# A hybrid decoder layer on one core: triangular inverses in seven small bundles instead of four, 16 narrow products a bundle in the preparation, another PSUM bank for the spatial gate, an undivided last tile, and other planner constants

## The chip, the cores and the metric

The kernel runs on one core of one Trainium2 chip. TensorE (PE) multiplies, VectorE (DVE) and ScalarE (ACT) work element by element and empty PSUM, GpSimd (POOL) does a few small things, and SyncE (SP) issues nearly all DMA transfers, in one queue and in program order. The metric is the device time of one execution in microseconds (us); the median of several runs counts, and less is better.

## What is computed

One layer of a decoder on 1024 tokens of width 2048: RMSNorm, one wide input projection, three groups that read its columns, an output projection, and a last RMSNorm. Cut to what matters here:

```python
h = rmsnorm(x, ln_g[l]);  proj = h @ w_in[l]          # 1024 x 2048 by 2048 x 6672
# group A: u * (tril(W_s) v + b) per chunk of 128 tokens, times silu(g_z)
s = jnp.einsum('gts,bcsgd->bctgd', w, v) + bs.T[None, None, :, :, None]
# group B: gated delta rule, 8 heads of 128, chunks of 64
a = jnp.where(strict, jnp.einsum('bhnid,bhnjd->bhnij', kb, k) * decay, 0.0)
T = lax.linalg.triangular_solve(a + eye, eye, left_side=True, lower=True, unit_diagonal=True)
value = jnp.einsum('bhnij,bhnjd->bhnid', T, vb)
_, o = lax.scan(step, s0, xs)                          # state carried from chunk to chunk
# group C: softmax attention of 4 heads into 256 memory tokens
mixed = jnp.concatenate([out_a, out_b, out_c], axis=-1)
return rmsnorm(x + mixed @ w_out[l], final_g)
```

What the change touches of this: the projection of h on the 16 columns d_a and d_b (the decays), the inverse T, the order in which group A and group B are worked, and the end of the output projection.

## The kernel before

**Wide products.** The input projection, the keys and values of the memory and the output projection are cut into pieces of 128 x 128 weights against 128 x 512 columns. Each float32 operand is split into a rounded high part and a rest (`lh`/`ll`, `lm` for the left side, `rhi`/`rlo` for the weights), and three products stand for one. The projections save products by a scheme with seven partial sums (`seven`, lines 1289 to 1348): sums and differences of two halves of the tokens (`hs_d`, `h0_d`, `hT_d`) against sums and differences of weight blocks. ACT makes `rhi` by a cast and DVE makes `rlo` by a subtraction, from `raw` (two buffers, filled by DMA) or from `kept` (four blocks that stay).

**Narrow products.** Two places use a fraction of the TensorE array. `prep1` (lines 825 to 853) handles the token tiles 4 to 7: it loads the rows of x into buffers named `kept`, `ut`, `states`, `steps` and `tblk`, scales and transposes them, forms the sums that the seven-sum scheme needs, and multiplies them with 32-column blocks of `abw` for d_a and d_b: 32 products for a token tile. `levels` (lines 1032 to 1107) builds the inverse of 32 triangular 128 x 128 matrices from inverses of their 32 x 32 diagonal blocks: 64 products of 32 x 32, then 96 more on the result of the first, then 32 of 64 x 64, then 32 more, with a copy out of PSUM after each. It runs twice, for the heads 0 to 3 (called a here) and 4 to 7 (b). Its results go to DRAM by small DMAs (`uhi`, `ulo`, `umid`), come back as `ut` (`load_u`, line 1109), and the scan of the delta rule (`scan_step`) multiplies with them.

**The order.** Nothing is issued as it is written. The kernel records every operation in a `Plan` (lines 63 to 397; all instructions carry the line 398, where the recorded calls are made), which lays them out engine by engine. `lay` runs the operations through a table of costs, taking on each engine the operation with the lowest key that is ready; `late` goes backwards from the end and gives each operation a due time, which is the key of the next pass; `issue` keeps the best of some passes and emits in that order. On the chip each engine then works its own list strictly in order. `together()` makes PE operations one bundle that nothing may split, `behind(op)` adds a dependence, and `rank` a class. STRETCH multiplies latencies on the way back, AHEAD says how far the modelled SP queue may run ahead of its transfers, PASSES counts the passes after the first.

**PSUM.** There are eight banks: `acc0` to `acc3` for the wide products, and `dn0` to `dn3` (dn_111 to dn_114 in the lists below) for the rest. The projection of the columns `zv` takes `acc` and dn2, dn3. `levels` takes dn0 and dn1, and `spatial` (the normalisation of group A's v, line 1620) takes dn1.

**The end.** The output projection's last bank is a tile of 128 tokens by 512 columns. Its last 24 products are made in two halves of 256 columns, so that the addition and the square sum of the first half run beside the products of the second; then `close` scales four column blocks and sends them out.

Of the kernel before, what the change touches and what calls it, by code (L numbers as in the profile page):

```python
# [17 lines left out]
P = 128  # L18
# [44 lines left out]
class Plan:  # L63
# [6 lines left out]
    FIRST, SPREAD, PASSES, STRETCH, AHEAD = 0, 1.75, 5, 1.0, 2000.0  # L70
# [112 lines left out]
    def price(self, o, name, outs, ins):  # L183
# [218 lines left out]
def kernel(  # L402
# [422 lines left out]
    def prep1(i):  # L825
# [20 lines left out]
        for q, (a, b, c, d, e) in enumerate(sets):  # L846
# [185 lines left out]
    def levels(gg, tdr, udr, n):  # L1032
# [19 lines left out]
        with rank(1):  # L1052
# [15 lines left out]
            for h in range(2):  # L1068
                turn_in(uhi[low(2 * h), :, low(0)], every(udr[64:96], h))
            with R.together():  # L1070
                for k in range(16):
                    for r in range(4):
                        t = tu[low(r), k] if r % 2 else tlo[low(r), k, low(0)]
                        PE.matmul(da[low(r), k], gc[low(r), k], t, start=True, stop=True)
            S.copy(yc, da)
            with R.together():
                for k in range(16):
                    for h in range(2):
                        r, q = low(2 * h), low(2 * h + 1)
                        PE.matmul(db[q, k], yc[r, k], tu[r, k], start=True, stop=True)  # L1080
                        PE.matmul(db[r, k], yc[q, k], uhi[q, k, low(1)], start=True, stop=True)
                        PE.matmul(da[q, k], tu[r, k], yc[r, k], start=True, stop=True)
            for h in range(2):
                S.copy(tlo[low(2 * h + 1), :, low(0)], da[low(2 * h + 1)])
                V.tensor_copy(uhi[low(2 * h), :, low(1)], db[low(2 * h)])
            S.copy(ux, db)
            sides = [(x_, h, w) for x_ in range(8) for h in range(2) for w in range(2)]
            with R.together():
# [73 lines left out]
    def heads_out(hf, hp, hss, rest):  # L1162
# [7 lines left out]
        for h, ob, bank in zip(hp, obs, scan_banks):  # L1170
# [4 lines left out]
            else:  # L1175
                e, y = sums(), ob.rearrange("p t c -> p (t c)")
# [112 lines left out]
    def seven(left, right, banks, takes, order, rows=False, last=False, first=0):  # L1289


        for n, key in enumerate(order):
# [3 lines left out]
            def product(t, i, a, ws, part=None, cols=None):  # L1296
                for u in range(2):
                    l, (hi, lo) = a[u], ws
                    o = bank[t]
                    if rows:  # L1300
                        l = [x_[:, t * P : (t + 1) * P] for x_ in l]
                        r = [x_[:, u * HT : (u + 1) * HT] for x_ in (hi, lo)]
                        if cols:
                            r, o = [x_[:, cols] for x_ in r], o[:, cols]
# [347 lines left out]
    tp = dnr.bufs[1]  # L1652
# [4 lines left out]
    tp = dnr.bufs[1]  # L1657
# [4 lines left out]
    for hf in range(2):  # L1662
        spatial(hf)
# [3 lines left out]
    el = over([abh[:, 0:HT], ring["tn"].bufs.pop()])  # L1667
    with rank(2.6):
# [107 lines left out]
    def total(r):  # L1776
        V.scalar_tensor_tensor(r[:, 4:5], r[:, 3:4], 1.0 / D, r[:, 4:5], op0=ALU.mult, op1=ALU.add)

    def close(half_, t):

        r, r0 = ssy[half_][t], half_ * HT + t * P
        total(r)
# [15 lines left out]
    def square(half_, t, c, cols=slice(0, HT)):  # L1798
        S.activation(jk[:, cols], ys[half_][t][c][:, cols], AF.Square, accum_out=ssy[half_][t][:, c : c + 1])
# [119 lines left out]
```

## Time and profile before

| | |
|---|---|
| median of 3 runs | 1586.66 us (1584.83 to 1587.31) |
| the profiled execution's own time | 1587.73 us |
| its span, first to last instruction | 1586.0 us |
| mean granted TensorE clock | 0.995 |
| DVE, ACT, POOL busy | 77%, 59%, 6% |
| DMA | 431.40 MB, mean 272 GB/s |

The span is what the trace shows; 1.73 us of the execution's own time lie around it. A matmul's duration in the trace is its time through the array; since matmuls are pipelined, the distance from one start to the next tells what one costs. The float32 products that are not rounded (32 x 32, 64 x 64, the `abw` blocks, transposes) appear as two or more records each.

### The profile page before, as it was taken

What the parts mean: (1) busy time and instruction counts of PE and PEld (TensorE: products, weight loads), DVE (VectorE), ACT (ScalarE), POOL (GpSimd) and SP (SyncE); (2) the same over time, 40 slices, a digit from 0 to 9 for tenths busy, and PEclk for the clock granted to TensorE, in tenths of its full rate; (3) what the DMA queues carried; (4) which work ended last, traced back from release to release, by engine and by line L of the source; (5) the groups of instructions that cost most, each with busy time, mean ns of one, the idle gap of its engine ahead of it and who ended that gap; (6) DMA issues with size and microseconds to landing.
All of it is one profiled execution on the core that took longest, in us unless ns stands there. A gap on an engine that the chain in (4) does not pass through costs nothing.

```text
span 1586.0 us, 25201 instructions
## 1 busy us (share of the span) xinstructions
PE 1559.0 (98%) x8773; PEld 1309.6 (83%) x8773; DVE 1219.6 (77%) x1802; ACT 931.7 (59%) x1921; POOL 102.1 (6%) x125
## 2 busy tenths in 40 slices
PE   8999999999999999999999999999999999999997
PEld 7987888888888778888888778888888888888886
DVE  6966844789979756887799667878668888688775
ACT  7832455767854247778864444876657864344455
POOL 0100001010020001110110010000000000000001
PEclk9999999999999999999999999999999999999999
DMA  9999866999988797886989896898868979678657
GB/s 328 305 333 330 288 182 201 323 324 336 301 260 275 236 294 245 263 282 193 276 275 319 240 261 218 279 343 284 257 211 267 310 263 351 214 269 294 227 151 274
DMA packets 338353, 431.40 MB, mean 272 GB/s; under 512 B 77353, under 2 KB 163890, under 8 KB 338226
## 3 DMA queue, kind: packets, MB, share of 16 engines
q1 hardware_dynamic: 336642, 427.09, 84.0%
q0 software_dynamic: 1088, 2.10, 0.4%
q8 instruction: 69, 1.13, 0.3%
q10 hardware_dynamic: 496, 0.61, 0.1%
q14 instruction: 58, 0.48, 0.1%
HBM read 330.29 MB, written 99.42 MB: 271 GB/s over the span
## 4 chain that ended last, share of the span: by engine, by line
PE 85%; DMA 4%; issue 1%; ACT 1%; DVE 1%; SPq 1%; POOLq 0%; POOL 0%; ACTq 0%; DVEq 0%
PE acc L398 53%; PE dn L398 32%; SPq L398 1%; DMA raw<-in_w_in_dram 1%; DMA E<-ed 1%; DMA late<-os 0%; DMA xr<-pd 0%; DMA kd<-late 0%; DMA ut<-uloa 0%; DMA ut<-in_x_dram 0%; DMA qT<-late 0%; DMA ll<-hsd 0%; ACT obs L398 0%; DVE tn L398 0%; ACT rhi L398 0%
## 5 line engine op out<-in xcount | busy, mean ns | idle before, releaser
L398 PE MATMUL acc<-lh,rhi 128*128 128x512 f32 x1024 | 396.6, 396 | 1.8 <-DVE obs L398 1.8
L398 PE MATMUL acc<-lh,rlo 128*128 128x512 f32 x1024 | 387.1, 396 | 0.2 <-DVE rlo L398 0.2
L398 ACT CAST rhi<-raw 128x1024 fp32r<-128x1024 f32 (+1 forms) x148 | 186.6, 1261 | 244.8 <-PE dn L398 119.3
L398 DVE TENSOR_TENSOR rlo<-raw,rhi 128x1024 fp32r<-128x1024 f32 (+1 forms) x148 | 219.3, 1482 | 106.6 <-ACT rhi L398 103.1
L398 PE MATMUL acc<-ll,rhi 128*128 128x512 f32 x688 | 269.9, 397 | 0.0
L398 PEld LDWEIGHTS acc<-lh,rhi 128*128 128x128 f32 x1024 | 193.3, 189 | 39.4 <-DVE obs L398 2.6
L398 PEld LDWEIGHTS acc<-lh,rlo 128*128 128x128 f32 x1024 | 193.0, 189 | 37.5 <-DVE rlo L398 0.7
L398 DVE TENSOR_TENSOR ll<-ll,lh 128x1024 fp32r<-128x1024 f32 x122 | 149.9, 1229 | 17.3 <-ACT lh L398 17.0
L398 PEld LDWEIGHTS acc<-ll,rhi 128*128 128x128 f32 x688 | 129.7, 189 | 24.8 <-DVE ll L398 0.2
L398 ACT CAST lh<-ll 128x1024 fp32r<-128x1024 f32 x122 | 127.9, 1048 | 23.2 <-DMA ll<-hsd 5.6
L398 PE MATMUL acc<-lm,rhi 128*128 128x512 f32 x336 | 133.4, 399 | 0.0
L398 PE MATMUL dn<-lh,rhi 128*128 128x512 f32 x288 | 112.9, 393 | 0.4 <-issue 0.4
L398 PE MATMUL dn<-lh,rlo 128*128 128x512 f32 x288 | 107.6, 393 | 0.0
L398 DVE TENSOR_TENSOR raw<-raw,kept 128x1024 f32<-128x1024 f32 (+1 forms) x56 | 81.1, 1452 | 3.6 <-DMA raw<-in_w_in_dram 3.6
L398 PE MATMUL dn<-ll,rhi 128*128 128x512 f32 x192 | 75.4, 394 | 0.0
L398 PEld LDWEIGHTS acc<-lm,rhi 128*128 128x128 f32 x336 | 63.6, 189 | 12.0
L398 DVE TENSOR_TENSOR rlo<-kept,rhi 128x1024 fp32r<-128x1024 f32 (+1 forms) x29 | 41.9, 1446 | 37.2 <-ACT rhi L398 37.1
L398 ACT CAST rhi<-kept 128x1024 fp32r<-128x1024 f32 (+1 forms) x29 | 35.7, 1230 | 51.4 <-PE dn L398 25.6
L398 POOL TENSOR_TENSOR hs<-hs,mhalf 128x4 f32<-128x4 f32 x32 | 45.8, 1436 | 273.7 <-DVE hs L398 262.6
L398 PEld LDWEIGHTS dn<-lh,rhi 128*128 128x128 f32 x288 | 54.3, 188 | 10.8
L398 PEld LDWEIGHTS dn<-lh,rlo 128*128 128x128 f32 x288 | 53.9, 188 | 10.4
L398 POOL TENSOR_TENSOR small<-small,mhalf 128x1 f32<-128x1 f32 x26 | 21.3, 819 | 580.7 <-DVE small L398 580.7
(412 smaller groups left out, 3395.8 us busy)
## 6 DMA issues: line engine op xcount, KB each, us to landing
raw<-in_w_in_dram SPq DMA_DIRECT2D x120, 512.0 KB
ll<-hsd SPq DMA_DIRECT2D x54, 512.0 KB
raw<-in_w_out_dram SPq DMA_DIRECT2D x48, 512.0 KB
raw<-in_w_in_dram SPq DMA_DIRECT2D x72, 256.0 KB
lm<-hsd SPq DMA_DIRECT2D x26, 512.0 KB
pd<-obs SPq DMA_DIRECT2D x48, 256.0 KB
late<-os SPq DMA_DIRECT2D x44, 256.0 KB
kept<-in_w_in_dram SPq DMA_DIRECT2D x20, 512.0 KB
```

The source lines that it names most:

```text
L398: o.fn(*o.args, **o.kw)
```

## The change

- **Inverses.** The four bundles of a `levels` (64, 96, 32 and 32 products) become seven of 32. The first 64 are halved, with a copy of half the bank after each half; the 96 are parted into three kinds, and each kind stands behind the copy of the one before it, so that other work can come between.
- **Preparation.** `prep1` closes its bundle after each half q: eight bundles of 16 in place of four of 32.
- **Spatial gate.** `spatial` and the transposes of its weights use dn2 instead of dn1, the names `scan_banks`, `hand`, `wide` and `el` are set before `spatial` runs, and `heads_out` takes its buffer from `E` instead of `sums`.
- **Last tile.** The last bank's products are 512 columns wide again; `close` computes the total by itself.
- **Planner.** PASSES 5 to 8, STRETCH 1.0 to 1.25, AHEAD 2000 to 1000, and a latency of 3500 more (FETCH) for products that are narrower than the array.

```diff
-    FIRST, SPREAD, PASSES, STRETCH, AHEAD = 0, 1.75, 5, 1.0, 2000.0
+    FIRST, SPREAD, PASSES, STRETCH, AHEAD = 0, 1.75, 8, 1.25, 1000.0
+    FETCH = 3500.0
...
-            o.lat = 175.0
+            o.lat = 175.0 + (0.0 if out.shape[0] == P or n == P or name == "transpose" else self.FETCH)
...
-        sets = [[pieces() for _ in range(5)] for q in range(2)]
-        for q, (a, b, c, d, e) in enumerate(sets):
+        for q in range(2):
+            a, b, c, d, e = (pieces() for _ in range(5))
...
-        with R.together():
-            for q, (a, b, c, d, e) in enumerate(sets):
+            with R.together():
                 for u, pair in enumerate(((c, a), (d, b))):
...
+            for e in range(2):
+                ks = slice(8 * e, 8 * e + 8)
+                with behind(R.ops[-1] if e else R.gate), R.together():
+                    for k in range(16)[ks]:
+                        for r in range(4):
+                            t = tu[low(r), k] if r % 2 else tlo[low(r), k, low(0)]
+                            PE.matmul(da[low(r), k], gc[low(r), k], t, start=True, stop=True)
+                S.copy(yc[:, ks], da[:, ks])
+            blocks = [(k, h, low(2 * h), low(2 * h + 1)) for k in range(16) for h in range(2)]
             with R.together():
-                for k in range(16):
-                    for r in range(4):
-                        t = tu[low(r), k] if r % 2 else tlo[low(r), k, low(0)]
-                        PE.matmul(da[low(r), k], gc[low(r), k], t, start=True, stop=True)
-            S.copy(yc, da)
-            with R.together():
-                for k in range(16):
-                    for h in range(2):
-                        r, q = low(2 * h), low(2 * h + 1)
-                        PE.matmul(db[q, k], yc[r, k], tu[r, k], start=True, stop=True)
-                        PE.matmul(db[r, k], yc[q, k], uhi[q, k, low(1)], start=True, stop=True)
-                        PE.matmul(da[q, k], tu[r, k], yc[r, k], start=True, stop=True)
+                for k, h, r, q in blocks:
+                    PE.matmul(da[q, k], tu[r, k], yc[r, k], start=True, stop=True)
             for h in range(2):
                 S.copy(tlo[low(2 * h + 1), :, low(0)], da[low(2 * h + 1)])
+            with behind(R.ops[-1]), R.together():
+                for k, h, r, q in blocks:
+                    PE.matmul(db[r, k], yc[q, k], uhi[q, k, low(1)], start=True, stop=True)
+            for h in range(2):
                 V.tensor_copy(uhi[low(2 * h), :, low(1)], db[low(2 * h)])
+            with behind(R.ops[-1]), R.together():
+                for k, h, r, q in blocks:
+                    PE.matmul(db[q, k], yc[r, k], tu[r, k], start=True, stop=True)
             S.copy(ux, db)
...
-            bank = dnr.bufs[1]
+            bank = dnr.bufs[2]
...
-                    if last and key == order[-1] and t == NT - 1:
-                        for cols in (slice(0, HT // 2), slice(HT // 2, HT)):
-                            for h in held:
-                                product(t, *h, cols=cols)
-                            takes[key](t, bank[t], cols)
-                        return
```

With other costs and constants the whole order changes, on every engine. Three places show it.

PE inside inverse a: before, the end of the bundle of 64, what stands between, and the start of the bundle of 96. The products of 32 x 32 read `gt`, `inv`; the wide ones write `acc`.

```order
L398 MATMUL dn_111<-gt_434,inv_432 32x32
L398 MATMUL dn_111<-inv_432 32x32
L398 MATMUL acc_110<-lh,rhi_76 128x512
L398 MATMUL acc_107<-lh,rhi_77 128x512
L398 MATMUL acc_107<-ll,rhi_77 128x512
L398 MATMUL acc_107<-lh,rlo_75 128x512
L398 MATMUL dn_112<-inv_432,inv_433 32x32
L398 MATMUL dn_112<-gt_435,inv_433 32x32
L398 MATMUL dn_111<-inv_433,inv_432 32x32
```

And now the same place, after the first bundle of 32, with the wide products in the middle left out:

```order
L399 MATMUL dn_111<-gt_434,inv_432 32x32
L399 MATMUL dn_111<-inv_432 32x32
L399 MATMUL acc_107<-lh,rlo_75 128x512
L399 MATMUL acc_107<-lh,rhi_77 128x512
L399 MATMUL acc_107<-lm,rhi_77 128x512
L399 MATMUL acc_107<-lh,rlo_75 128x512
...
L399 MATMUL dn_113<-lm,rhi_77 128x512
L399 MATMUL dn_113<-lh,rlo_75 128x512
L399 MATMUL dn_111<-gt_434,inv_432 32x32
L399 MATMUL dn_111<-inv_432 32x32
```

Four wide products stood between two bundles, now 18; between the other bundles of a and b there stand 18 to 25 products, nearly all of them wide (before 4 or 8 wide ones). After the last bundle of inverse a, 57 wide products and 8 of 128 columns stood before the first product of the scan that reads `ut`; now 73 and 8. After inverse b they were 434 and 64 (the spatial gate and more lay between), now 70 and 21.

DVE in the preparation, where the reduction for the row scale of the last token tile (`small_100`, which needs that tile's rows of x in `ut`) stands among the writes out of the transposes of the tile before it (`tn_86`, `tn_87`, `kT_350`, `kd_121` from the bank dn_112). Before:

```order
L398 TENSOR_TENSOR tn_86<-dn_112,gcol_130 128x512
L398 TENSOR_REDUCE small_100<-small_100 128x1
L398 TENSOR_SCALAR small_100<-small_100 128x1
L398 TENSOR_TENSOR rlo_75<-raw_73,rhi_77 128x1536
L398 TENSOR_TENSOR tn_87<-dn_112,gcol_130 128x512
L398 TENSOR_SCALAR ut_82<-ut_82,small_100 128x512
L398 TENSOR_TENSOR kT_349<-tn_86,tn_87 128x512
L398 TENSOR_SCALAR ut_83<-ut_83,small_100 128x512
L398 TENSOR_TENSOR kT_350<-dn_112,gcol_130 128x512
```

Now:

```order
L399 TENSOR_TENSOR tn_86<-dn_112,gcol_130 128x512
L399 TENSOR_TENSOR tn_87<-dn_112,gcol_130 128x512
L399 TENSOR_TENSOR kT_349<-tn_86,tn_87 128x512
L399 TENSOR_TENSOR rlo_74<-raw_72,rhi_76 128x1536
L399 TENSOR_TENSOR tn_86<-tn_88,tn_86 128x512
L399 TENSOR_TENSOR kT_350<-dn_112,gcol_130 128x512
L399 TENSOR_TENSOR tn_88<-kT_349,tn_88 128x512
L399 TENSOR_REDUCE small_100<-small_100 128x1
L399 TENSOR_TENSOR tn_89<-tn_89,tn_88 128x512
L399 TENSOR_TENSOR kd_121<-dn_112,gcol_130 128x512
```

The reduction stood ahead of three of the four writes out of that bank, now ahead of one. On SP the last of these rows of x is issued after 37.6 MB of transfers, before after 39.2 MB. On PE the narrow products of `prep1` form seven runs, not eight, since the first two bundles follow each other directly.

PE at the very end. Before, the last bank's first products, in half width:

```order
L398 MATMUL dn_114<-rlo_74,fh_521 128x512
L398 MATMUL dn_114<-rhi_76,fl_519 128x512
L398 MATMUL dn_111<-oh 128x256
L398 MATMUL dn_111<-rs,oh 128x256
L398 MATMUL dn_111<-oh,lm 128x256
```

Now:

```order
L399 MATMUL dn_114<-rhi_76,fl_519 128x512
L399 MATMUL dn_111<-rhi_77,ll 128x512
L399 MATMUL dn_111<-oh 128x512
L399 MATMUL dn_111<-rs,oh 128x512
L399 MATMUL dn_111<-oh,lm 128x512
```

24 products of 256 columns became 12 of 512.

More of the change, by code (lines that the diff above doesn't have):

```diff
@@ L1085, in levels @@
+            for h in range(2):
                 V.tensor_copy(uhi[low(2 * h), :, low(1)], db[low(2 * h)])
+            sides = [(x_, h, w) for x_ in range(8) for h in range(2) for w in range(2)]
+            with behind(R.ops[-1]), R.together():
+                for k, h, r, q in blocks:
+                    PE.matmul(db[q, k], yc[r, k], tu[r, k], start=True, stop=True)
             S.copy(ux, db)
-            sides = [(x_, h, w) for x_ in range(8) for h in range(2) for w in range(2)]
-            with R.together():
+            with behind(R.ops[-1]), R.together():
@@ L1294, in seven, with product @@
             bank = banks(key)
-            def product(t, i, a, ws, part=None, cols=None):
+            def product(t, i, a, ws, part=None):
                 for u in range(2):
@@ L1651 @@
     Q.dma_start(wt, gmlp_ws[0].rearrange("g t s -> t g s"))
-    tp = dnr.bufs[1]
+    tp = dnr.bufs[2]
     for g in range(NG):
@@ L1656 @@
         V.tensor_tensor(out=wsT[g], in0=tp[:, g * P : (g + 1) * P], in1=utri, op=ALU.mult)
[L1657 removed]
+    tp = dnr.bufs[2]
     for g in range(NG):
@@ L1661 @@
         V.scalar_tensor_tensor(bt[g], tp[:, sl], col2[:, 4 + g : 5 + g], bsb[:, sl], op0=ALU.mult, op1=ALU.add)
-    for hf in range(2):
-        spatial(hf)
     scan_banks = dnr.bufs[0:2]
@@ L1667 @@
     el = over([abh[:, 0:HT], ring["tn"].bufs.pop()])
+    for hf in range(2):
+        spatial(hf)
     with rank(2.6):
@@ L1846, in final, with take @@
             put = more(m, key, after)
-            def take(t, a, cols=slice(0, HT)):
-                r = ssy[key[0]][t]
-                if cols.stop - cols.start < HT:
-                    add(y[key][t][:, cols], a[:, cols], y[key][t][:, cols])
-                    square(key[0], t, c, cols)
-                    total(r) if cols.start == 0 else close(key[0], t)
-                    return
+            def take(t, a):
                 put(t, a)
                 square(key[0], t, c)
+                r = ssy[key[0]][t]
                 if c == 3:
```

13 lines of the change are left out of this document (4 added, 9 removed).

## The prediction

> **What bounds the kernel now.** First I read the page's busy shares and its chain of waits:
>
> ```profile
> PE 1559.0 (98%) x8773; PEld 1309.6 (83%) x8773; DVE 1219.6 (77%) x1802; ACT 931.7 (59%) x1921; POOL 102.1 (6%) x125
> PE 85%; DMA 4%; issue 1%; ACT 1%; DVE 1%; SPq 1%; POOLq 0%; POOL 0%; ACTq 0%; DVEq 0%
> ```
>
> PE is the bound, and nothing in the change takes wide products away. In an undisturbed stretch 24 of them take 5.44 us, 0.227 us each:
>
> ```profile
> 480.60 5.44 PE acc L398 x24
> ```
>
> So only PE's idle time, time at a lower clock, and the price of the narrow bundles can move. Second view: what PE waited for, in the whole run and in the windows of the two inverses (540 to 600, 890 to 930 us).
>
> ```profile
> PE dn L398 <- issue: 5.8, 5, 2.4
> PE dn L398 <- DMA ut<-uloa: 2.7, 1, 2.7
> PE acc L398 <- DVE obs L398: 1.8, 1, 1.8
> PE dn L398 <- DVE tn L398: 1.7, 1, 1.7
> ...
> PE dn L398 <- issue: 1.5, 2, 1.1
> ...
> PE dn L398 <- issue: 4.2, 3, 2.4
> ```
>
> All of the waiting on "issue" (1.5 + 4.2 = 5.7 us) lies in the two inverses: PE is held up by nothing that another engine does. The timeline of PE shows where, first in a, then in b:
>
> ```profile
> 554.84 0.21 PE L398 MATMUL dn<-gt,inv 32*32 32x32 f32 x1 [1.09 <-issue]
> 564.47 0.39 PE L398 MATMUL dn<-lh,rhi 128*128 128x512 f32 x1 [0.43 <-issue]
> ...
> 902.76 0.21 PE L398 MATMUL dn<-inv,inv 32*32 32x32 f32 x1 [2.40 <-issue]
> 908.95 1.16 PE L398 MATMUL dn<-gt,ut 64*64 64x64 f32 x64 [1.15 <-issue]
> 913.01 0.34 PE L398 MATMUL dn<-gt,inv 64*64 64x64 f32 x5 [0.70 <-issue]
> ```
>
> Third view: windows from the end of one such wait to the end of the next, and over the stretches at a lower clock.
>
> ```profile
> 902.75:908.94 6.19, 5.05 (x128) 3.70 (x128) 3.17 (x4) 1.74 (x3) 0.00 (x0) 0.72 0.85 267
> 908.94:913.00 4.06, 3.36 (x127) 2.70 (x127) 1.82 (x2) 2.48 (x3) 0.96 (x1) 1.00 0.65 189
> 554.84:564.46 9.62, 9.19 (x254) 7.15 (x255) 4.04 (x6) 3.55 (x7) 0.96 (x1) 0.82 1.04 325
> ...
> 556.18:559.59 3.41, 3.41 (x10) 2.46 (x8) 2.06 (x3) 1.74 (x3) 0.00 (x0) 0.50 1.06 344
> 580.08:583.49 3.41, 2.93 (x9) 2.57 (x10) 1.02 (x2) 0.96 (x3) 0.10 (x1) 0.50 1.17 262
> 904.34:907.75 3.41, 3.41 (x8) 2.16 (x8) 2.60 (x3) 1.67 (x3) 0.00 (x0) 0.50 0.88 259
> ```
>
> From wait to wait PE ran 128, 127 and 254 = 2 x 127 products, each with its weight load (the PEld column has as many). That is a supply that arrives in portions of 128 and needs 6.19, 4.06 and 9.62 / 2 = 4.81 us for one; wide products use a portion in 128 x 0.227 = 29 us, narrow ones in about 1. I read the waits as instruction supply. The last three rows show a second price: PEclk 0.50 for 3.41 us after each of these pile-ups and after the wait for `ut`, 1.7 us of lost work each.
>
> A sentence of the Trainium skill fits the portion: "Runtime: NRT & Kernel Launch", section "Instruction fetch mechanics", says that instructions are refilled in blocks of 256, which is 128 products with their weight loads. The same section calls the crossing of a block mostly hidden; by it the 5.7 us would have another cause and would stay (a rival below). The trace agrees on the block and not on the hiding.
>
> **The change part by part.** The sum starts from the profiled execution's own time, 1587.73 us (span 1586.0 plus 1.73 around it), which is 1.07 above the median.
>
> *Supply waits: -5.7.* Now each run is 32 products (64 records) followed by 18 to 25, nearly all wide: about 83 records in 0.55 + 20 x 0.227 = 5.1 us. At the slowest portion seen, 128 in 6.19 us, 105 would arrive in that time. So the supply keeps up. Bounds: 0 (nothing helps) and -5.7; I take -5.7, since 83 lies clearly under 105.
>
> *Clock: -3.4.* The two half-clock stretches behind these waits (556.18 and 904.34) cost 2 x 1.7. With half a microsecond of narrow work in 5 us PE looks like the rest of the run. Bounds 0 and -3.4; they go with the waits.
>
> *More bundles: +3.0.* A bundle costs something on entry and exit:
>
> ```profile
> 550.02 0.39 PE L398 MATMUL acc<-lh,rlo 128*128 128x512 f32 x1
> 550.34 0.21 PE L398 MATMUL dn<-gt,inv 32*32 32x32 f32 x1
> ...
> 551.44 0.19 PE L398 MATMUL dn<-inv 32*32 32x32 f32 x1
> 551.56 0.73 PE L398 MATMUL acc<-lh,rhi 128*128 128x512 f32 x2
> 552.13 0.39 PE L398 MATMUL acc<-ll,rhi 128*128 128x512 f32 x1
> ```
>
> In: 0.32 to the first narrow start instead of 0.227, 0.09 more. Out: 0.12, and the next two wide products take 0.57 instead of 0.45, 0.12 more. Together 0.33 us, with 0.4 as the upper bound for `abw` bundles, whose shape differs. There are 2 x 3 more in the inverses and 3 more in the preparation, nine in all: 9 x 0.33 = 3.0 (at most 3.6). This is paid on PE, with nothing beside it. The Trainium skill says the same against the change ("TensorEngine Tiling (Array Packing)", "Key Properties": a change of tiling mode drains the array) but gives no price; the trace's 0.33 is used.
>
> *Copies in the inverses.* One more PSUM copy and a longer row of hand-overs in each inverse. They lie beside 18 to 25 other products, so they cost PE nothing; without that cover each of the three added hand-overs would cost a copy of about 0.7 us:
>
> ```profile
> 561.02 0.69 DVE L398 COPY inv<-dn 128x512 f32<-128x512 f32 x1 [1.97 <-PE dn L398]
> ```
>
> *Scan behind the inverse: -3.4.* The result has to go out to DRAM and return before the scan.
>
> ```profile
> 563.08 0.50 PE L398 MATMUL dn<-lh,rlo 128*128 128x512 f32 x1
> ...
> 580.56 0.77 PE L398 MATMUL dn<-vs,ut 128*128 128x128 f32 x2 [2.70 <-DMA ut<-uloa]
> ```
>
> From the end of the last bundle to `ut` it took 580.56 - 563.08 = 17.5 us, and the 57 + 8 products in between did not fill it: 2.70 of wait and 1.7 of half clock, 4.4 in all. The new order puts 73 x 0.227 = 16.6 us there and 8 products of 128 columns, at most 0.60 / 4 = 0.15 each (the rows of x4 below): 16.6 to 17.8, about enough. But the scan now follows inverse b as closely: 70 x 0.227 and 21 smaller ones, 15.9 to 19.0 us (before 434 wide ones, so no wait there). Bounds: both covered, -4.4; both as bad as the one now, -4.4 + 8.8 = +4.4. I take half a microsecond of wait at each and no half clock, since the shortest wait that left half clock here was 1.09 us: -4.4 + 1.0 = -3.4.
>
> *Preparation: -1.7.* PE waited 1.72 us here (the chain of waits, first row, and the timeline):
>
> ```profile
> 119.00 5.78 DMA ut<-in_x_dram
> ...
> 125.62 0.16 DVE L398 TENSOR_REDUCE small<-small 128x1 f32<-128x4 f32 x1 [2.01 <-ACT jk L398]
> 128.67 0.68 DVE L398 TENSOR_TENSOR tn<-dn,gcol 128x512 f32<-128x512 f32 x1
> 129.41 0.66 PE L398 MATMUL dn<-ident,states 128*128 128x128 f32 x4 [1.72 <-DVE tn L398]
> 143.88 0.60 PE L398 MATMUL dn<-ident,ut 128*128 128x128 f32 x4
> ```
>
> DVE stood at the reduction for the last tile until its x had landed at 124.8, with `rlo` and the write `tn` queued behind it, for which PE waited to transpose again into that bank. The tile itself was wanted by PE only at 143.88, 19 us later. In the new order three of the four writes stand ahead of the reduction, and the last of x is issued after 37.6 MB instead of 39.2, which at 39.2 MB in 124.8 us is 5 us earlier. By the count of products ahead of it the preparation's last bundle comes 14 us of PE work earlier, so of the 19 us some 10 remain. Bounds: -1.7, and +1.7 (the wait stays and a second one joins it at the last write). I take -1.7, as the reduction's place in the queue was the cause.
>
> *Last tile: -0.7.* Before:
>
> ```profile
> 1573.84 0.28 PE L398 MATMUL dn<-oh 128*128 128x256 f32 x1
> ...
> 1576.18 0.39 PE L398 MATMUL dn<-oh 128*128 128x256 f32 x1 [0.74 <-DVE kd L398]
> ...
> 1577.59 0.28 PE L398 MATMUL dn<-rhi,fl 128*128 128x256 f32 x1
> 1577.91 0.42 DVE L398 TENSOR_TENSOR kd<-dn,kd 128x256 f32<-128x256 f32 x1
> 1578.72 0.42 ACT L398 ACTIVATE jk<-kd 128x256 bf16<-128x256 f32 x1 [0.53 <-DVE kd L398]
> ```
>
> The second half had to wait until the first was added out of the same bank. First to last start: 3.75 us; undivided 11 x 0.227 = 2.50, 1.25 earlier. Behind it the whole-tile steps are longer (rows for 512 columns):
>
> ```profile
> 1574.04 0.69 DVE L398 TENSOR_TENSOR kd<-dn,kd 128x512 f32<-128x512 f32 x1 [0.72 <-PE dn L398]
> 1574.83 0.63 ACT L398 ACTIVATE jk<-kd 128x512 bf16<-128x512 f32 x1
> ```
>
> 0.11 for the last product (0.39 against 0.28), 0.27 for the addition, 0.21 for the squares: +0.59. Net -0.66.
>
> *Bank of the spatial gate, `E`, planner constants: +4.0.* These have no price of their own: they move everything. The waits outside the inverses' "issue" are, start and end left aside, 2.7 + 1.8 + 1.7 and little else, so this order is good; a new one has waits of its own at other places. I have credited 1.7 and 3.4 for waits that go, and set +4.0 for ones that come; bounds 0 and +12, twice all the waits named here.
>
> Sum: -5.7 - 3.4 + 3.0 - 3.4 - 1.7 - 0.7 + 4.0 = -7.9, so 1579.8 for a profiled execution and, 1.07 lower, a median of about 1579.
>
> **Rivals.**
>
> *Both scans wait (slower).* The transfers of the inverses' last level stand in SP's queue behind writes that wait for DVE, and at b now also behind the spatial gate's. If a result takes longer than the middles of these stretches, 17.2 us at a and 17.5 at b, PE waits, and all behind it on PE. With one more transfer time on that way, like the 5.78 us of x in the preparation, it takes 23.3: waits of 6.1 + 1.7 at a and 5.8 + 1.7 at b, 15.3, less the 4.4 of now, +10.9 in place of -3.4. The median becomes about 1593. For it: 17.5 against 17.2 is no margin. Against: the results of the middle levels are now sent earlier.
>
> *The supply waits stay* (they belong to the modes, or 32 products are still too many): no -5.7 and no -3.4, about 1588, which cannot be told from no change. Against it: the portions of 127 and 128.
>
> *The new order has no new waits*: +4.0 falls away, and so does the wait for `obs` of 1.8 behind inverse b: about 1573.
>
> **How the numbers follow.** Forecast 0.55, no new waits 0.15, supply stays 0.12, both scans wait 0.18. Anything within 0.2% (3.2 us) cannot be told from no change: faster is below 1583.5. The forecast gives 0.51 of its 0.55 to faster and 0.04 to same; no new waits is faster; supply stays is same (0.09) or slower (0.03); both scans wait is slower. Faster 0.66, same 0.13, slower 0.21. All the best ends together give 1587.7 - 5.7 - 3.4 + 3.0 - 4.4 - 1.7 - 1.3 - 1.8 - 1.1 = 1571; the range reaches from a little below it, 1569, to the slower rival, 1593.
>
> **What would show it.** In the new profile the waits on "issue" should be near zero at the inverses and no 0.50 clock should stand there before the end; the bundles should show 0.33 us around each. A wait `ut` behind inverse a or b of more than 2 us, with half clock behind it, would show the slower rival. "issue" waits that stay, with 127 or 128 products between them, would refute the supply's balance; ones at other counts, the supply itself. A wait on `tn` or `kd` in the first 150 us would show the preparation wrong, and new waits on DVE or DMA of more than 10 us together the +4.0.

## The result and the profile after

| | before | after |
|---|---|---|
| median, same chip | 1587.19 us (1584.83 to 1589.31, 5 runs) | 1575.80 us (1574.23 to 1581.16, 5 runs) |
| ratio, 95% interval | | 0.9937 [0.9918, 0.9956] |
| the profiled execution's own time | 1587.73 us | 1575.80 us |
| its span | 1586.0 us | 1573.9 us |

The change makes the kernel faster by 11.4 us, or 0.6%, and the interval excludes a ratio of 1; about 1579 was predicted, with a range of 1569 to 1593. First the page of after: busy shares, the chain of waits, and one DMA queue to which we come back.

```profile
PE 1556.8 (99%) x8761; PEld 1307.4 (83%) x8761; DVE 1216.3 (77%) x1800; ACT 934.3 (59%) x1925; POOL 94.3 (6%) x125
PE 97%; DMA 1%; DVE 1%; issue 1%; ACT 1%; POOLq 0%; POOL 0%; ACTq 0%; SPq 0%; DVEq 0%
q8 instruction: 69, 1.13, 0.3%
```

The chain that ended last is PE's own work for 97% of the span, before for 85%. What is left between PE's products, in the view of waits (total us, times, longest):

```profile
PE dn L399 <- DMA y<-in_mem_norm_g_dram: 2.9, 1, 2.9
PE dn L399 <- issue: 1.7, 1, 1.7
PE dn L399 <- DMA kept<-in_mem_dram: 1.5, 1, 1.5
PE dn L399 <- ACT rhi L399: 1.0, 1, 1.0
PE dn L399 <- DVE states L399: 0.8, 1, 0.8
PE acc L399 <- ACT yu L399: 0.3, 1, 0.3
PE dn L399 <- ACT jk L399: 0.2, 1, 0.2
```

The waits on `y`, `kept` and `rhi` are the start of the kernel and stood in before as well. Those on `tn` and `obs` are gone, and "issue" is down from 5.8 in five to one of 1.7. The two inverses by windows, before and then after (columns: us, busy time of PE, PEld, DVE, ACT, POOL, granted clock, DMA share, GB/s):

```profile
549.00:567.00 18.00, 16.48 (x486) 12.86 (x485) 4.05 (x7) 5.72 (x9) 0.96 (x1) 0.91 0.94 260
896.00:914.00 18.00, 13.76 (x472) 10.53 (x472) 7.13 (x8) 6.43 (x9) 1.00 (x2) 0.91 0.82 216
```

```profile
540.10:578.00 37.90, 37.90 (x519) 30.56 (x519) 17.59 (x19) 11.93 (x14) 0.95 (x1) 1.00 1.01 313
924.00:965.00 41.00, 40.97 (x597) 32.50 (x596) 25.68 (x35) 21.95 (x32) 5.33 (x7) 1.00 0.81 227
```

An inverse is now stretched over more than twice the time, PE is busy in all of it, and the clock is 1.00 instead of 0.91. In the whole span of after no stretch at half clock is left but the one at the end.

The one "issue" that remains lies at the scan behind inverse a (timeline of PE):

```profile
572.38 1.16 PE L399 MATMUL dn<-gt,inv 64*64 64x64 f32 x64
...
590.88 0.39 PE L399 MATMUL dn<-lh,rhi 128*128 128x512 f32 x1
...
593.00 0.68 PE L399 MATMUL dn<-vs,ut 128*128 128x128 f32 x4 [1.73 <-issue]
```

Its name misleads. The product reads `ut`, the inverse's result, which comes in packets under 512 bytes; the DMA view of 592.0 to 592.5 and of 592.5 to 592.9 us shows when they stop:

```profile
DMA packets 147, 0.10 MB, mean 191 GB/s; under 512 B 114, under 2 KB 114, under 8 KB 147
...
DMA packets 41, 0.08 MB, mean 196 GB/s; under 512 B 3, under 2 KB 3, under 8 KB 41
```

The last of them ends at about 592.6, and PE starts at 593.00. So this is the wait for the result's way through DRAM, 1.73 us.

### The profile page after: what moved, and what is told of

Read it like the earlier page. It is cut to its first block, busy times and chain, and to the rows that moved or that the text cites. A ratio compares the mean times of both kernels' runs of the same rounds, so it can differ in the third digit from the quotient of the medians.

```text
span 1573.9 us, 25104 instructions
## 1 busy us (share of the span) xinstructions
PE 1556.8 (99%) x8761; PEld 1307.4 (83%) x8761; DVE 1216.3 (77%) x1800; ACT 934.3 (59%) x1925; POOL 94.3 (6%) x125
## 3 DMA queue, kind: packets, MB, share of 16 engines
q8 instruction: 69, 1.13, 0.3%
## 4 chain that ended last, share of the span: by engine, by line
PE 97%; DMA 1%; DVE 1%; issue 1%; ACT 1%; POOLq 0%; POOL 0%; ACTq 0%; SPq 0%; DVEq 0%
PE acc L399 59%; PE dn L399 38%; DMA raw<-in_w_in_dram 1%; ACT rhi L399 0%; DMA kept<-in_mem_dram 0%; DVE lm L399 0%; DVE raw L399 0%; DVE states L399 0%; ACT jk L399 0%; DVE inv L399 0%; ACT lh L399 0%; ACT vs L399 0%; DVE os L399 0%; ACT obs L399 0%; DVE kd L399 0%
## 5 line engine op out<-in xcount | busy, mean ns | idle before, releaser
L399 PE MATMUL acc<-lh,rlo 128*128 128x512 f32 x1024 | 380.2, 394 | 0.0
L399 PEld LDWEIGHTS acc<-lm,rhi 128*128 128x128 f32 x336 | 63.2, 188 | 11.9
L399 DVE TENSOR_TENSOR lm<-lm,lh 128x1024 fp32r<-128x1024 f32 x42 | 51.1, 1218 | 7.3 <-ACT lh L399 7.3
```

What stands on the lines that cost most here:

```text
L399: o.fn(*o.args, **o.kw)
```

## What the instruction queue shows

The page has a DMA queue for instructions, q8. Its 69 transfers are 1.13 MB / 69 = 16.4 KB each, and 8761 products with as many weight loads, shared among 69, are 254 instructions or 127 products: one transfer is one of the prediction's portions. The count can be made exact with the semaphore instructions that PE's queue holds as well: the stops of before at 902.76, 908.95 and 913.01 us stand at its instructions 10689, 10945 and 11201, 256 apart each time. All 15 waits on "issue" in before and in experiments 1, 3, 4 and 5 stand at 192 or 193 past a multiple of 256; no other wait of PE in the fourteen kernels does. Three windows of the kernel before: 900.3 to 901.3, 902.76 to 906.5 and 906.5 to 907.6 us.

```profile
q8 instruction: 1, 0.02, 6.0%
...
q1 hardware_dynamic: 1316, 1.29, 98.9%
...
q8 instruction: 1, 0.02, 5.6%
```

PE starts on one portion at 902.76 and runs dry within the next few microseconds, but for 3.8 us nothing comes on q8: the kernel's own transfers on q1 hold 98.9% of the DMA engines. The portion passes at 906.59 to 907.57, and PE goes on at 908.95. The trace has every transfer's time; some of them, with the products counted from border to border:

| kernel, inverse | PE enters a portion | the next passes on q8 | PE enters it | wait "issue" |
|---|---|---|---|---|
| before, b | 902.76 | 906.59 to 907.57 | 908.95 | 1.15 |
| before, b | 908.95 | 910.58 to 911.55 | 913.01 | 0.70 |
| experiment 1, a | 561.27 | 565.58 to 566.51 | 567.84 | 0.92 |
| experiment 3, a | 571.44 | 577.43 to 578.53 | 580.09 | 4.39 |
| experiment 5, a | 552.91 | 556.58 to 557.51 | 558.83 | 4.34 |

Every one of these waits ends 1.3 to 1.6 us after its transfer. The transfer itself takes 0.9 to 1.1 us, and it starts 1.6 to 6.0 us after PE entered the portion before. So a portion costs 4.1 to 8.7 us in these narrow stretches, and only one is fetched ahead: PE stands still when it gets through 128 products in less. In all fourteen traces PE enters no portion sooner than 1.3 us after its transfer. That the late starts come from the kernel's own data is likely but not shown: q1 held 96% and more of the DMA engines in the four long ones (3.7 to 6.0 us) and 82% in the short one.

The Trainium skill, "Runtime: NRT & Kernel Launch", section "Instruction fetch mechanics", describes an engine that fetches blocks of 256 instructions over a DMA queue of its own. The trace agrees on both. That crossing a block is mostly hidden holds here where wide products fill a block (29 us) or thin the narrow ones out, as in after, and not in before's inverses.

## The experiments

The kernel before ran beside each; on these chips its medians were 1583.6 to 1586.1 us, so ratios are compared. Single runs of one kernel spread over up to 8 us, so that a profiled run can stand 4 us from its kernel's median: the profiles of 1 and 12 are among the fastest of their twelve runs (1580.87 against a median of 1584.84, 1581.53 against 1584.28), that of 10 is the slowest of six (1581.09 against 1578.00).

**1. The seven bundles alone** (before, with the change's lines in `levels` and the old constants):

```diff
+            for e in range(2):
+                ks = slice(8 * e, 8 * e + 8)
+                with behind(R.ops[-1] if e else R.gate), R.together():
...
+            with behind(R.ops[-1]), R.together():
+                for k, h, r, q in blocks:
+                    PE.matmul(db[r, k], yc[q, k], uhi[q, k, low(1)], start=True, stop=True)
```

> The kernel before, with only the seven smaller bundles in the two inverses and the old planner constants: the bundles are 7 x 64 records with only 3 to 7 wide products between two of them. Supply theory (portions of 128 products, one in 4.1 to 6.2 us): 448 narrow and some 31 wide records would take PE about 11 us; in the kernel before the first wait came after 204 to 213 records, so some 270 are left, 2.1 portions, 8.5 to 13 us: 1.5 to 5 us of wait on issue in each inverse, with 127 or 128 products from one to the next, and a stretch of half clock behind the longest. Time 1584 to 1593, no gain over before. Rival (it is the length of a bundle or the number of levels in one mode that stops PE): no issue wait in either inverse, and 1587.2 - 5.7 - 3.4 + 2.0 (six more entries and exits) = about 1580.

Measured: ratio 1.0005 [0.9996, 1.0014]. The timeline, and the windows from wait to wait:

```profile
561.27 0.31 PE L398 MATMUL dn<-inv,inv 32*32 32x32 f32 x8 [0.93 <-issue]
567.84 0.34 PE L398 MATMUL dn<-inv,inv 32*32 32x32 f32 x10 [0.92 <-issue]
572.73 0.39 PE L398 MATMUL dn<-gt,inv 64*64 64x64 f32 x10 [0.28 <-issue]
910.99 0.33 PE L398 MATMUL dn<-gt,inv 64*64 64x64 f32 x6 [0.57 <-issue]
```

```profile
561.26:567.83 6.57, 5.65 (x128) 4.34 (x127) 4.15 (x6) 1.16 (x2) 0.00 (x0) 1.00 1.03 364
567.83:572.72 4.89, 4.61 (x127) 3.44 (x127) 1.29 (x2) 1.18 (x2) 0.96 (x1) 1.00 1.03 288
```

Small bundles do not end the waits: 128 and 127 products again. The 2.1 us in a were expected (1.5 to 5), the 0.6 in b are less, and no half clock followed in this profile. Its mean clock was 0.999, that of the eleven other runs 0.994 to 0.997, so they may well have had some. The rival, no such wait and a gain of 7 us, is out.

**2. No spacing** (after, FETCH at 0):

```diff
-    FETCH = 3500.0
+    FETCH = 0.0
```

> The kernel after, with the constant FETCH at 0, so that the planner puts only 3 to 11 wide products between the seven bundles of an inverse in place of 18 to 25. Supply theory: the issue waits come back, 1 to 5 us in each inverse, 127 or 128 products (or a multiple) from one to the next, and with them up to 1.7 us of half clock each: 1575.8 + 3 to 12 = 1579 to 1588. Rival (small bundles alone were enough): no issue wait in the inverses, 1575.8 within 3.

Measured: 1.0003 [0.9994, 1.0012], the whole gain lost, but with no wait on issue: the supply theory missed the kind of wait and the rival the time. The view of waits has others:

```profile
PE dn L399 <- DMA vd<-sm: 3.2, 1, 3.2
...
PE dn L399 <- DVE gt L399: 2.5, 2, 1.3
```

PE now waits 1.3 and 1.1 us for the copies between two bundles, and 3.2 behind inverse b, at the first product that reads its `ut`. While PE waits for the copies, portions pass: three of them end 1.4 to 1.5 us before their border is crossed, just in time, as in the table. So the spacing has two jobs, to let portions come and to cover the copies; here the waits for the copies seem to hide those for the portions. What the spacing alone is worth against the supply, this run does not show.

**3. Spacing alone** (after, with the old four bundles):

```diff
+                for k in range(16):
+                    for r in range(4):
...
+                        PE.matmul(db[q, k], yc[r, k], tu[r, k], start=True, stop=True)
+                        PE.matmul(db[r, k], yc[q, k], uhi[q, k, low(1)], start=True, stop=True)
```

> The kernel after, with the four bundles of before in each inverse (128, 192, 64 and 64 records), but the planner's spacing kept: 19 to 25 wide products between two. Supply theory: the stock at the start held 204 to 213 records in the kernel before, and 4.3 us pass between the first two bundles, about one portion; so 128 + 19 + 192 = 339 records meet a stock of some 205 and one portion more, 333: at most one short wait in each inverse, 0 to 2 us, at the end of the second bundle. Six entries and exits fewer give back 2.0 us. Time 1572 to 1579. Rival (the length of a bundle is what counts): a wait of 1 to 2.4 us stays in the bundle of 192 of both inverses, with half clock behind it, 1575.8 - 2.0 + 2 x (1.1 to 2.4 + 1.7) = 1579 to 1582.

Measured: 0.9976 [0.9966, 0.9986], slower than after. Inverse a has one long wait, b none. The row, and then the windows of the portion ahead of it and of the like one in b:

```profile
580.09 0.25 PE L399 MATMUL dn<-gt,inv 32*32 32x32 f32 x1 [4.39 <-issue]
```

```profile
571.43:580.08 8.65, 4.27 (x129) 3.40 (x127) 0.69 (x1) 0.00 (x0) 0.00 (x0) 0.86 0.99 304
944.50:951.52 7.02, 5.92 (x152) 4.76 (x141) 2.26 (x4) 2.12 (x3) 0.33 (x1) 1.00 0.58 159
```

Neither expectation fits whole. My count of a stock and portions on top was wrong: what counts is where the borders fall. In a, one portion held 12 wide products and 116 narrow ones and was gone in 4.1 us, while the next needed 8.7 with DMA at 0.99. In b a border fell into the first bundle, the next portion had the wide products and a wait for `inv` in it, and arrived in time. (The 152 of that row count also the records under way at its ends; from start to start it is 128.)

**4. The kernel before with the new constants:**

```diff
-    FIRST, SPREAD, PASSES, STRETCH, AHEAD = 0, 1.75, 5, 1.0, 2000.0
+    FIRST, SPREAD, PASSES, STRETCH, AHEAD = 0, 1.75, 8, 1.25, 1000.0
+    FETCH = 3500.0
...
+            o.lat = 175.0 + (0.0 if out.shape[0] == P or n == P or name == "transpose" else self.FETCH)
```

> The kernel before with the planner constants of after (FETCH among them) and nothing else: bundles of 128, 192, 64 and 64 records with 19 to 28 wide products between two. Supply theory: the issue waits of 5.7 us fall to 0 to 2 in all and both half-clock stretches in the inverses go, 1587.2 - 5.7 - 3.4 = 1578, with up to 4 us for what the redrawn order does elsewhere: 1576 to 1584. Rival (it is the bundles' length): the waits stay, 1585 to 1590.

Measured: 1.0034 [1.0022, 1.0046], slower than before; a miss. Both bundles of 192 records break:

```profile
551.47 0.26 PE L399 MATMUL dn<-inv,inv 32*32 32x32 f32 x2 [2.31 <-issue]
894.63 0.26 PE L399 MATMUL dn<-inv,inv 32*32 32x32 f32 x2 [3.28 <-issue]
```

A bundle of 192 can hold a whole portion, and the spacing around it did not help here. That is the sense in which the length of a bundle counts: not by itself, but against 128. The redrawn order also brought waits of 7.0 us elsewhere, 3.8 of them for `ll` at 424 us.

**5 and 6. The borders moved by half a portion,** in before and in after: 64 records more at the start, nothing else moved. The 32 products are work that neither kernel has otherwise.

```diff
+    with rank(0), R.together():
+        for k in range(32):
+            PE.matmul(dnr.bufs[1][0:32, 32 * (k % 16) : 32 * (k % 16) + 32], ident[0:32, 0:32], ident[0:32, 0:32], start=True, stop=True)
```

> The kernel before with 32 narrow products more (64 records of 32 x 32, about 1.1 us of PE, their result is not used) at the very start, everything behind them in the old order: each block border of 128 products falls 64 records earlier in the program, so half a block away from where it was. Supply theory: the waits on issue leave their places (products 81 and 72 of the second bundle) and come where the borders now are: at products 15 and 143 of the second bundle of inverse a and, with a fetch of 3.9 to 6.6 us for a block that PE goes through in 2.7 and 1.3 us, they are longer: 4 to 11 us in each inverse, 8 to 20 in all in place of 5.8, ratio to before 1.002 to 1.010. Rival (the waits belong to the bundles or their modes): the waits stay at products 81 and 72 with their lengths, ratio 1.000 to 1.001.

> The kernel after with the same 32 narrow products (result not used) at the start and the order else unchanged. Supply theory: a block in its inverses takes PE 7 to 12 us wherever the borders fall, longer than the 3.9 to 6.6 us of most fetches: no wait on issue in the inverses or one of at most 1.5 us; ratio to before 0.9937 + 0.0007 = 0.9944, within 0.002. Rival (the change was lucky with its borders): waits of 2 us and more with half clock behind them, ratio 0.997 to 1.001.

Measured: 1.0015 [1.0005, 1.0025] and 0.9952 [0.9938, 0.9966]. The waits of the shifted kernel before, and the window between the first two:

```profile
552.91 0.21 PE L398 MATMUL dn<-inv,inv 32*32 32x32 f32 x2 [0.67 <-issue]
558.83 0.21 PE L398 MATMUL dn<-inv,inv 32*32 32x32 f32 x1 [4.34 <-issue]
904.72 0.26 PE L398 MATMUL dn<-inv,inv 32*32 32x32 f32 x2 [4.76 <-issue]
```

```profile
552.90:558.82 5.92, 1.58 (x128) 1.46 (x128) 0.00 (x0) 0.00 (x0) 0.00 (x0) 0.94 1.02 330
```

The waits moved with the borders, in a to products 17 and 145 of the second bundle (15 and 143 expected, 81 before), in b to 136 (72 before), and grew from 5.8 to 9.8 us. This is the clearest of the runs: the same bundles, copies and order, and only the borders elsewhere. A price of the bundles or of their modes cannot move so. The time rose less than expected, as the wait for `ut` behind a fell from 2.70 to 0.65 meanwhile and the added products fit into a wait at the start. The shifted kernel after has no wait in its inverses and none for `ut`:

```profile
PE dn L399 <- DMA sm<-gvd: 0.6, 1, 0.6
PE acc L399 <- ACT yu L399: 0.3, 1, 0.3
PE dn L399 <- ACT jk L399: 0.2, 1, 0.2
```

Bundles of 64 records with some 20 wide products between held in both positions of the borders, and in the other orders below.

**7. Spatial gate as before** (bank, buffer and place in the program), and **9. its bank alone:**

```diff
-            bank = dnr.bufs[2]
+            bank = dnr.bufs[1]
...
-    tp = dnr.bufs[2]
+    tp = dnr.bufs[1]
```

> The kernel after with the spatial gate on its old bank, its old place in the program and the old buffer for its factor. Theory (the bank has no price of its own, it only lets the order be drawn otherwise): no issue waits in the inverses, waits at other places of 0 to 6 us, ratio 0.992 to 0.998. Rival (the bank of its own is what lets the scan follow inverse b closely and spares the wait for obs): that wait of 1.8 us comes back and others with it, ratio above 0.998.

> The kernel after with the spatial gate's products on the old bank and nothing else undone. The planner draws another order with it: between inverse b and the scan stand again some 460 wide products, behind inverse a 14.2 us of products. Supply theory: seven bundles with 19 to 27 wide products between, so no wait on issue over 1.5 us in either inverse. Waits of the order: the result of an inverse took 14.8 to 19.6 us from the last bundle to the scan in the runs so far, so 0.6 to 5 us of wait behind a, none behind b; and waits at other places as in the orders seen so far, 3 to 15 us in all. If the bank is what made the run with three things undone slow, the ratio is above 1.002; if it was that one order, 0.992 to 1.000.

Measured: 1.0074 [1.0060, 1.0089] and 1.0054 [1.0039, 1.0070]. The first was too slow for my theory, and its rival's mechanism did not come either: no wait on `obs`. In the second the bank is all that was undone, and it is enough. Its largest waits:

```profile
PE dn L399 <- ACT os L399: 7.0, 2, 3.5
...
PE acc L399 <- ACT rhi L399: 2.0, 1, 2.0
PE dn L399 <- ACT kd L399: 1.0, 1, 1.0
```

They lie at 393 and 403, at 67 and at 415 us, ahead of inverse a and far from the spatial gate: the planner drew another order, with a some 50 us earlier in PE's work and b 112 us of products ahead of its scan. All three kernels that have the old bank and the new constants (4, 7 and 9) wait for ACT or DVE between 360 and 435 us, none of the others does for 0.2 us.

**8. The last tile in halves** (after, with before's loop over `cols`):

```diff
+                        for cols in (slice(0, HT // 2), slice(HT // 2, HT)):
+                            for h in held:
+                                product(t, *h, cols=cols)
+                            takes[key](t, bank[t], cols)
```

> The kernel after with the last tile in two halves of its columns as before, the order of all else unchanged. Theory: from the first product of the last tile to the end of the span 12.18 us as in the kernel before, against 11.52 in after, +0.66, with the wait for the first addition of 0.74 back; ratio 0.9937 + 0.0004. Rival (the halves do not matter or help, as they let the last steps start earlier): 11.5 or less.

Measured: 0.9957 [0.9940, 0.9974]. From the first product of the last tile to the end 1572.93 - 1561.01 = 11.92 us, with this wait in it:

```profile
1563.35 0.39 PE L399 MATMUL dn<-oh 128*128 128x256 f32 x1 [0.74 <-DVE kd L399]
```

In five halved kernels that stretch takes 11.9 to 12.2 us, in the nine whole ones 11.5 to 11.8: whole is better by 0.4 or a little more; the ratio is too coarse for that.

**10, 11 and 12. One other edit undone each:** the factor's buffer, the preparation, and the three old constants beside FETCH.

```diff
-                e, y = ring["E"](), ob.rearrange("p t c -> p (t c)")
+                e, y = sums(), ob.rearrange("p t c -> p (t c)")
```

```diff
-        for q in range(2):
-            a, b, c, d, e = (pieces() for _ in range(5))
+        sets = [[pieces() for _ in range(5)] for q in range(2)]
+        for q, (a, b, c, d, e) in enumerate(sets):
```

```diff
-    FIRST, SPREAD, PASSES, STRETCH, AHEAD = 0, 1.75, 8, 1.25, 1000.0
+    FIRST, SPREAD, PASSES, STRETCH, AHEAD = 0, 1.75, 5, 1.0, 2000.0
```

> The kernel after with only the factor of the spatial gate in its old buffer. Another order of the planner, with inverse and scan as in after: 16.3 us of products behind inverse a, 18.4 behind b. No wait on issue over 1.5 us in the inverses; behind a 0 to 3 us of wait, behind b 0 to 1. If the order matters only by its waits, the ratio is 0.9937 plus the waits outside issue above the 3.0 us of after (each us 0.0006); if the buffer has no effect of its own, 0.992 to 0.998. Rival (the old buffer holds up the gate): a wait at the gate of over 2 us and a ratio above 0.998.

> The kernel after with the preparation as before, four bundles in place of eight. 15.1 us of products stand behind inverse a, 17.8 behind b. Theory: four bundles fewer save 4 x 0.33 = 1.3 us, but the reduction stands ahead of the writes in DVE's queue again, so a wait of 1 to 2.5 us comes in the first 150 us (on tn or another of DVE's results); 0 to 4 us of wait behind inverse a; ratio 0.993 to 0.997. Rival (the preparation's bundles have nothing to do with that wait): no wait of DVE in the first 150 us and a ratio of 0.993 or lower.

> The kernel after with PASSES, STRETCH and AHEAD of before, FETCH kept: the smallest change of the planner, a new order with 18.1 us of products behind inverse a and 16.9 behind b. No wait on issue over 1.5 us in the inverses. If after has an order that is better than such orders mostly are, waits outside issue of 4 to 10 us where after has 3.0, and 0.9937 + 0.0006 for each us above: 0.994 to 0.999. If the waits of after are what such orders mostly have, 0.9925 to 0.9945.

Measured: 0.9943 [0.9927, 0.9959], 0.9943 [0.9928, 0.9959] and 0.9990 [0.9978, 1.0001]. None waits on issue. The buffer and the preparation cannot be told from nothing; the three constants are worth half a per cent, of which the waits below explain 1.8 us; where the rest comes from stays open. In 11 the wait on `tn` did not come back, and DVE's queue agrees:

```profile
120.02 0.68 DVE L399 TENSOR_TENSOR kT<-dn,gcol 128x512 f32<-128x512 f32 x1
120.62 0.14 DVE L399 TENSOR_REDUCE small<-small 128x1 f32<-128x4 f32 x1
```

The reduction stands behind three of the four writes here too, with bundles of 32. And 10, which has the eight bundles, waits 2.2 us for `small` at 89 us.

All orders together (5, 6 and 8 keep the order of before or of after). "Other waits" are PE's, without "issue" at the borders and without the start, and the last column counts stretches of 3.41 us at half clock before the end. The ratio is of many runs, the other columns are of one profiled run, which for 1 and 12 was a fast one:

| kernel | ratio | issue, us | other waits, us | half clock |
|---|---|---|---|---|
| before | 1 | 5.8 | 7.8 | 3 |
| after | 0.9937 | 0 | 3.0 | 0 |
| 1 seven bundles alone | 1.0005 | 2.7 | 3.6 | 0 |
| 2 no spacing | 1.0003 | 0 | 7.7 | 2 |
| 3 spacing alone | 0.9976 | 4.4 | 4.3 | 2 |
| 4 before, new constants | 1.0034 | 5.6 | 7.0 | 4 |
| 7 gate as before | 1.0074 | 0 | 14.6 | 5 |
| 9 bank as before | 1.0054 | 0 | 12.8 | 5 |
| 10 buffer as before | 0.9943 | 0 | 4.3 | 1 |
| 11 preparation as before | 0.9943 | 0 | 4.0 | 1 |
| 12 three constants as before | 0.9990 | 0 | 4.8 | 0 |

No run beat after.

## Why the prediction was right, point by point

*Supply waits, -5.7.* 5.8 became 0. The cause is shown, by q8 and by the borders moved. The picture of a balance, so many records per microsecond, was good enough for after; the exact rule is one portion ahead, and experiments 3 and 4 missed where I had counted by the balance.

*Clock, -3.4.* Both stretches are gone: 0.91 became 1.00 in the windows above.

*More bundles, +3.0.* PE's narrow runs went from 12 to 21, nine more, and the way in and out of each costs what was read:

```profile
548.55 0.39 PE L399 MATMUL acc<-lh,rhi 128*128 128x512 f32 x1
548.87 1.20 PE L399 MATMUL dn<-inv,inv 32*32 32x32 f32 x64
550.00 0.50 PE L399 MATMUL acc<-ll,rhi 128*128 128x512 f32 x1
550.33 0.40 PE L399 MATMUL acc<-lh,rlo 128*128 128x512 f32 x1
550.57 0.39 PE L399 MATMUL acc<-lh,rhi 128*128 128x512 f32 x1
```

0.32 on the way in; 0.57 for the next two wide starts on the way out, as before. But the term left out what is inside. These 64 records take 1.13 us to the next wide start, three such bundles 3.39; undivided, in inverse b of experiment 3, the same 192 records took 2.25 (window from the first of them to the next wide start):

```profile
950.51:952.76 2.25, 2.25 (x192) 2.21 (x192) 1.08 (x4) 0.00 (x0) 0.55 (x1) 1.00 1.09 356
```

Less 0.12 for each exit that is 3.03 against 2.13: parted into three kinds, the 96 products of an inverse take 0.9 us longer, 1.8 in both. Why was not tried. So this term measured about +4.8 instead of +3.0.

*Scan behind the inverse, -3.4.* The half clock went (1.7), and of the wait 1.73 stayed instead of 0.5; b has none. Measured -2.7. The order of after gives this wait in one run and not in others (experiments 6 and 8), so half a microsecond of cover is a coin's toss.

*Preparation, -1.7.* The size is right: the wait is gone. The reason held half-way: the place of the reduction in DVE's queue fits, but in experiment 11 the redrawn order puts it there without the smaller bundles.

*Last tile, -0.7.* First product of the tile to the end of the span: 12.18 before; after, from these two rows, 2.50 and 9.02 us, 11.52 in all.

```profile
1562.40 0.39 PE L399 MATMUL dn<-oh 128*128 128x512 f32 x1
...
1564.90 0.39 PE L399 MATMUL dn<-rhi,fl 128*128 128x512 f32 x1
```

*Bank, buffer and constants, +4.0.* This is the term that was mis-sized most. The waits that went besides those credited are `obs` 1.84, `os` 0.40, `rlo` 0.23 and `vs` 0.20, 2.7 in all; those that came are `states` 0.82, `yu` 0.28 and `jk` 0.16, 1.3 in all: -1.4 instead of +4.0. With the measured terms, -5.8 - 3.4 + 4.8 - 2.7 - 1.7 - 0.7 - 1.4 = -10.9, against -11.9 between the two profiled executions, although after also waits 0.3 longer for `kept` at the start: some 1.3 us of the gain stay unexplained. That the forecast came within 3.2 us of the median is in part luck: 5.4 too much here stood against 1.8 too little for the bundles and 0.7 for the scan.

The step that was off priced a new order by the waits of the one at hand. By the prediction's terms 7.8 - 1.7 - 1.7 - 0.7 + 4.0 = 7.7 us of other waits should have been left. Six orders with the same bundles in the inverses and FETCH (after, 7, 9, 10, 11, 12) have 3.0, 14.6, 12.8, 4.3, 4.0 and 4.8, on the mean 7.3: the sum was right for an average that no order has. Their waits fall in two groups, by the bank of the spatial gate, to which the prediction gave no price of its own. Undone, it costs 1.0054 / 0.9937, 1.2% or some 18 us, more than the whole gain; 12.8 - 3.0 = 9.8 us more of other waits and five stretches of half clock at 1.7 make 18.3. Each side rests on a few drawn orders, and why the planner's orders with the old bank are so much worse was not tried.

Of the rivals, "no new waits" came nearest (1573, and `obs` gone), but with the `ut` wait. "Both scans wait" did not happen: b's result was in time. "The supply waits stay" is refuted for after, and true for the parts of the change alone.

## What to carry to other kernels

Long runs of tiny TensorE products can be limited by instruction delivery: compare the time that PE takes for each 128 products with what a portion needs while the DMA engines are full (4.1 to 8.7 us here), and put enough wide work between short runs that no alignment of the borders matters. Two edits can each be worth nothing alone and pay only together, here small runs (experiment 1) and spacing (experiment 4), though each run also drew a new order; so test them together before dropping either. Where a planner draws the order, an edit with no cost of its own can move it by more than the edit that was meant to help: price it from several drawn orders, not from one.

## What the runs showed that was not expected

- The instruction fetch appears among the DMA queues and has no right of way that shows here: 3.7 to 6.0 us from PE's entering a portion to the next one's start on q8, where q1 held 96% of the DMA engines and more.
- A wait that the trace calls "issue" can be a late transfer: the 1.73 us at 593.00, told apart by the packets' ends and by standing 20 instructions past a portion's border.
- Half clock does not follow from the length of a wait alone. 1.09 us amid narrow products left 3.41 us of it; waits of 1.73 in after and 1.99 in experiment 1, amid wide ones, left none. The Trainium skill, "TensorE: Matmul & The Clock Gate", section "What's actually happening", tells of a free-running window of 3413 ns; the stretches here are all of that length or twice and four times it, which agrees. Within each trace all changes of the clock lie on one grid of 3.41 us, and on it the waits can be told apart. In the fourteen traces, start and end left aside, every window of the grid in which PE stood for 1.77 us or more was followed by half clock; none with 1.73 or less was, unless it held narrow bundles or was itself at half clock. The 1.99 us fell on a border of the grid, 0.4 on one side and 1.6 on the other. So how a wait lies on the grid decides together with its length, and by this the same wait can cost 1.7 us more in one run than in the next.
